# Own tiles for the retention outputs, four raw weight slots of 4 KB, and a bias table read backward in a two-layer decoder trunk

## The chip, the cores and the metric

The kernel runs on one core of a Trainium2 chip. The metric is the device time of one launch in microseconds (us), from runs on the chip. Besides those runs one execution was recorded by the hardware profiler; the times of single instructions below come from that one. The engines have short names there: PE does matmuls (PEld loads their stationary operand), DVE is the vector engine, ACT the scalar engine, POOL the general one, and SP here only issues DMAs.

## The reference

Two layers; each mixes 512 tokens of width 1024 by three causal branches (differential attention with a relative-position bias, chunked retention, a gated short convolution), gates and sums them, projects and adds; then a gated feed-forward part with a causal convolution. Cut to what the change touches:

```python
def layer(l, x):                                    # x: (512, 1024) float32
    h = rmsnorm(x, norm_mix_g[l])
    q, k, v, rq, rk, rv, rg, sb, sc, sx, gates = split(h @ w_in[l])
    # differential attention: 4 heads, 2 maps of 64 columns each, values of 128 columns
    s = q @ k.T + bias_dist[max(i - j, 0)]          # per head and map; masked where j > i
    a = softmax(s[map 0]) - lam * softmax(s[map 1])
    o_da = rmsnorm(a @ v, da_subln_g[l]) * (1 - lam_init)
    # retention: 4 heads in chunks of 128 tokens, decay per head
    o_ret = rmsnorm(retention(rotary(rq), rotary(rk), rv), ret_norm_g[l]) * silu(rg)
    o_sc = sb * causal_conv(sc * sx)
    y = sum(sigmoid(gates[b] + b_gate[b]) * (o_b @ w_branch_b) for b, o_b in enumerate((o_da, o_ret, o_sc)))
    x = x + y @ w_out[l]
    g, u = split(rmsnorm(x, norm_ffn_g[l]) @ w_ffn_in[l])
    return x + (silu(causal_conv(g)) * u) @ w_ffn_out[l]
```

`bias_dist` has one value for each distance and head; it comes from a table of 32 buckets that both layers share.

## The kernel before

**Numbers.** Every matrix product is computed from float32 operands split into a rounded part `hi` and a remainder `lo` (type float32r). One product is three matmuls: hi by hi, hi by lo, lo by hi (`mm3`, L157 to L161). A weight tile is loaded by SP into a slot of the tag "raw" (`load_w`), copied by ACT to `hi` (L150) and subtracted by DVE to `lo` (L151) (`split_w`); the slot is free again when DVE has read it. Two raw slots of 8 KB per partition exist, whatever the size of the load.

**Slots.** Tiles with one tag share a fixed number of slots in SBUF; a new tile takes the slot that comes free and its first writer waits for the last reader of the tile before. The tag "N" has nine slots (`NN`) of 4 KB and holds, over the mixing part of a layer, most of what lives long: the natural-order queries and keys of a head (`nat`), its values split in two (`v`), its transposed queries (`q`) and keys (`k`), the outputs of the heads (`om`), of retention (`omr`) and of the short convolution (`oms`), and retention's own operands (`rv`, `rT`, `knh`, `knl`). PSUM has eight banks, four under the tag "main" (projections and branch products) and four under "aux" (transposes, scores, values).

**The work of a layer.** `mix` first computes two projections of 1024 columns in natural order (`pnrqk`, `pnrvg`), then runs two things woven into each other. One is a filler of plain matmuls (`filler`): for each head h its projection into the four main banks (`pnh0` to `pnh3`, `head_chunk`), with short-convolution and gate products between them (`ptsc`, `ptg`), and the branch products `pb`. `evacuate` empties the four banks of a head: ACT copies queries and keys to `nat` (L432), squares them in place (L433) and writes the high part of the values `v` (L169), and DVE writes their low part (L170) and a row sum (L435, `msqk`). The other is attention and retention, step by step: for a block i of 128 queries the scores `pS0hi` and `pS1hi` (map 0 and 1 of head h; L487, L488), on DVE the addition of the bias with the minimum over the row (L492), on ACT the exponential (L493), on DVE the difference of the two maps, on PE the transposition `pThi` (L511), its split into `aT` by ACT (L166) and DVE (L167), and on PE the products with the values, into `po0h` for blocks 0 and 1 and `po2h` for blocks 2 and 3 (L523, L524). When the four blocks of head h are done, their normed sum `o` is transposed (`ptoh`) and stored as `om[h]`. For retention `por` stands for the products with the values and `PT` for its transposed scores.

The names in the profile carry no buffer numbers, and the names in the order rows below do (`pnh3L_2044`); in `po02` the first digit is the block and the second the head, in `pS123` the digits are map, head and block, in `pT20` head and block, and L ends the name of the tile of a layer.

**The order of instructions** on each engine is set by the framework's scheduler when the kernel is built: it takes the instructions in an order of priorities and of its own estimate of when operands and slots come free. `high_priority` puts weight loads and splits early. So a change of slots changes the order in which the engines do their work, though the source is the same. SP, POOL and each other engine then work strictly in that order: an instruction that waits holds all that is behind it on its engine.

**The bias table.** `biases` (once) builds on PE one line of 640 values per head by a product of the 32 buckets with a one-hot matrix, stores it in DRAM (`line`) and then writes it 128 times into a DRAM table `skew`, by a DMA that POOL issues (L224). `tables` (each layer) loads from `skew`, with a row pitch one shorter, the tile `bias_t`: for each query row of a block and each head 512 biases, descending in distance from left to right. The scores of block i add its last (i+1)·128 columns.

**The feed-forward part** has 22 tiles of 128 columns, in groups of 5, 9 and 8. The first group (`plain`) loads 1 MB per tile and uses it in two halves, every second block of 512 columns for g, the others for u. The other two groups (`seven`) use seven products of quarter size, for which DVE builds sums of the weight quarters (`s31`, `s24`).

Of the kernel before, what the change touches and what calls it, by code (L numbers as in the profile page):

```python
# [11 lines left out]
F32 = mybir.dt.float32  # L12
F32R = mybir.dt.float32r
I32 = mybir.dt.int32
AF = mybir.ActivationFunctionType
ALU = mybir.AluOpType
# [10 lines left out]
H = 4  # L27
# [26 lines left out]
def trunk(ctx, tc, xT, wr, wh, wt, wda, wret, wsc, wo, wf, w2, par, lamp, relb, onehot, mask, rope, gtab, out):  # L54
# [76 lines left out]
        return i  # L131

    def load_w(src, name):
        n = src.shape[1]
        with tc.high_priority():
            raw = wp.tile([P, n], F32, tag="raw", bufs=2, name="raw_" + name, padded_shape=[P, 2 * D])
            ordered(nc.sync.dma_start(raw, src))
        return raw

    def split_w(raw, name):  # L140
# [64 lines left out]
        nc.sync.dma_start(gtab_t, gtab)  # L205
        nc.sync.dma_start(mask_t, mask)

    skew = dr.tile([H, P * 640], F32, name="skew")

    def biases():  # L210

        rb = cp.tile([BUCKETS + 1, 16], F32, name="rb")[:, :H]
        V.memset(rb[BUCKETS : BUCKETS + 1], -BIG)
        G.dma_start(rb[:BUCKETS], relb)
        line = dr.tile([H, 640], F32, name="line")
        for a, b in ((0, 512), (512, 640)):
            oh = temp(f"oh{a}", b - a)[: BUCKETS + 1]
            G.dma_start(oh, onehot[:, a:b])
            ps = aux(f"psb{a}")
            T.matmul(ps[:H, : b - a], rb, oh, start=True, stop=True)  # L220
            row = temp(f"line{a}", b - a)[:H]
            V.tensor_copy(row, ps[:H, : b - a])
            G.dma_start(line[:, a:b], row)
        G.dma_start(skew.rearrange("h (p n) -> h p n", n=640), line.unsqueeze(1).broadcast_to([H, P, 640]))  # L224


    pads = [cp.tile([P, S + 2], F32, name=f"pad{i}") for i in range(2)]
# [71 lines left out]
    def mix(l, mp):  # L299
# [11 lines left out]
        for t in qz:  # L311
            G.memset(t.bitcast(F32), 0.0)

        def tables():

            src = skew[:, 127 : 127 + 639 * P].rearrange("h (p n) -> p h n", n=639)
            G.dma_start(bias_t, src[:, :, :S])

        lam_init = 0.8 - 0.6 * math.exp(-0.3 * l)

# [130 lines left out]
        def attention(h):  # L451
# [27 lines left out]
            def scores(i):  # L479
                W = (i + 1) * P  # L480
                nm = f"{h}{i}{L}"
                qs = slice(i * P, (i + 1) * P)
                z = small(2, f"z{nm}")
                e = []
                pS2 = [aux(f"pS{m}{nm}") for m in range(2)]
                for m in range(2):
                    T.matmul(pS2[m][:, :W], qs2[:, m, qs], kh2[:, m, :W], start=True, stop=False)  # L487
                    T.matmul(pS2[m][:, :W], qs2[:, m, qs], klz[:, m, :W], start=False, stop=True)  # L488
                for m, pS in enumerate(pS2):
                    s_ = temp(f"s{m}{nm}", W)  # L490
                    mn = small(1, f"mn{m}{nm}")
                    V.tensor_tensor_reduce(s_, pS[:, :W], bias_t[:, h, S - W : S], 1.0, 3.0e38, ALU.add, ALU.min, mn)  # L492
                    A.activation(s_, s_, AF.Exp, bias=mn, scale=-1.0, accum_out=z[:, m : m + 1])  # L493
                    e.append(s_)
                st_[i].update(z=z, e=e)
# [63 lines left out]
        def retention(p):  # L559
# [83 lines left out]
            yield  # L643
            yield
            ps = transposes(lambda st: o[:, st * P : (st + 1) * P], f"ptor{p}{L}")
            om[4 + p] = split2(ps, pairN(f"omr{p}{L}"), pt[:, G_RET : G_RET + 1])
            yield


# [91 lines left out]
    def ffn(l, fp):  # L741
# [28 lines left out]
            split(flat(t), flat(X[k][:, 0, 3:7]), flat(X[k][:, 1, 3:7]))  # L770

        def plain(f):
            raw = load_w(wf[l, f], f"f{L}{f}").rearrange("p (b n) -> p b n", n=S)
            ps = main(f"pg{f}{L}")
            project(xg, ps, split_w(raw[:, 1::2], f"fg{L}{f}"))
            if not norm:
                norm.append(norm_x(f"f{L}")[1])
            padt = pads[f % 2]
            V.tensor_tensor(padt[:, 2 : S + 2], ps, norm[0], ALU.mult)
            c = temp(f"c{f}{L}")  # L780
            wc = FF_W + 3 * f
            conv(c, padt, lambda t: pt[:, wc + t : wc + t + 1], pt[:, FF_B + f : FF_B + f + 1])
            A.activation(c, c, AF.Silu)
            ps = main(f"pu{f}{L}")
            project(xg, ps, split_w(raw[:, 0::2], f"fu{L}{f}"))
            u = temp(f"u{f}{L}")
            V.tensor_tensor(u, ps, norm[0], ALU.mult)
            V.tensor_tensor(u, u, c, ALU.mult)
            return split2(u, pairN(f"act{f}{L}"))

        def seven(f):
            raw = load_w(wf[l, f], f"f{L}{f}")
            r4 = raw.rearrange("p (b n) -> p b n", n=S)
            a11, a12 = r4[:, 1], r4[:, 3]
            with tc.high_priority():
                w11 = split_w(raw[:, S : 2 * S], f"fa{L}{f}")
                s31 = fp.tile([P, 2, S], F32, tag="sum", name=f"s31{f}{L}", bufs=2)
                V.tensor_tensor(s31, r4[:, 0:1].broadcast_to([P, 2, S]), r4[:, 1:3], ALU.add)
                h31, l31 = slotX(f"h31{f}{L}"), slotX(f"l31{f}{L}")
                split(s31, h31, l31)  # L800
                s24 = fp.tile([P, 2, S], F32, tag="sum", name=f"s24{f}{L}", bufs=2)
                V.tensor_tensor(s24[:, 0], s31[:, 1], a11, ALU.add)
                V.tensor_tensor(s24[:, 1], s24[:, 0], a12, ALU.add)
                h24, l24 = slotX(f"h24{f}{L}"), slotX(f"l24{f}{L}")
                split(s24, h24, l24)
                w2212 = split_w(raw[:, 2 * S : 4 * S], f"fb{L}{f}")
            w22, w12 = [tuple(t[:, b * S : (b + 1) * S] for t in w2212) for b in range(2)]

            def product(o, w, b, start, stop):
                for k in range(KT // 2):  # L810
                    sl = slice(k * P, (k + 1) * P)
                    mm3(o, (w[0][:, sl], w[1][:, sl]), (X[k][:, 0, b], X[k][:, 1, b]), start and k == 0, stop and k == KT // 2 - 1, True)

            a = main(f"pa{f}{L}")[:, :HALF]
            b = main(f"pb{f}{L}")
            padt = pads[f % 2]
            u = temp(f"u{f}{L}")
            product(a, w11, 0, True, True)
            A.copy(padt[:, 2 : HALF + 2], a)
            product(b[:, HALF:], (h31[:, 1], l31[:, 1]), 3, True, True)  # L820
            A.copy(u[:, HALF:], b[:, HALF:])
            product(a, (h24[:, 0], l24[:, 0]), 4, False, True)
            A.copy(padt[:, HALF + 2 : S + 2], a)
            product(b[:, HALF:], (h24[:, 1], l24[:, 1]), 2, False, True)
            product(a, (h31[:, 0], l31[:, 0]), 5, False, True)
            V.tensor_tensor(u[:, HALF:], u[:, HALF:], a, ALU.add)
            product(b[:, :HALF], w12, 1, False, True)
            V.tensor_tensor(padt[:, 2 : S + 2], padt[:, 2 : S + 2], b, ALU.add)
            product(a, w22, 6, False, True)
            A.copy(u[:, :HALF], a)  # L830
            c = temp(f"c{f}{L}")
            wc = FF_W + 3 * f
            conv(c, padt, lambda t: pt[:, wc + t : wc + t + 1], pt[:, FF_B + f : FF_B + f + 1])
            A.activation(c, c, AF.Silu)
            V.tensor_tensor(u, u, c, ALU.mult)
            return split2(u, pairN(f"act{f}{L}"))
# [34 lines left out]
def _consts():  # L871

    f = np.float32
    onehot = np.zeros((BUCKETS + 1, 640), f)
    half = BUCKETS // 2
    for n in range(640):
        dist = 511 - n
        if dist < 0:
            onehot[BUCKETS, n] = -1.0
            continue  # L880
        b = dist
        if dist >= half:
            b = half + int(math.log(dist / half) / math.log(MAX_DIST / half) * (BUCKETS - half))
            b = min(b, BUCKETS - 1)
        onehot[b, n] = -1.0
    inv = (f(10000.0) ** (-np.arange(32, dtype=f) / f(32))).astype(f)
    ang = (np.arange(S, dtype=f)[:, None] * inv[None, :]).astype(f).astype(np.float64)
    cs, sn = np.cos(ang), np.sin(ang)
    table = np.stack([np.concatenate([cs, cs], 1), np.concatenate([-sn, sn], 1)], 0).astype(f)
    rope = np.ascontiguousarray(table.reshape(2, ST, P, 64).transpose(2, 0, 1, 3))  # L890

    mask = (np.arange(P)[None, :] >= np.arange(P)[:, None]).astype(f)
    pos = np.arange(S, dtype=np.float64)
    gtab = np.zeros((P, ST, 4, 2), f)
    for c in range(4):
        for b in range(2):
            g = np.float64(np.log1p(-(2.0 ** (-5.0 - (2 * (c % 2) + b)))))
            col = np.exp(g * pos) if c < 2 else np.exp(-g * pos) / 8.0
            gtab[:, :, c, b] = col.reshape(ST, P).T
    return onehot, mask, rope, gtab.reshape(P, ST, 8)  # L900
# [74 lines left out]
```

## Time and profile before

| what | value |
|---|---|
| median of 3 runs | 1548.77 us (1547.65 to 1552.67) |
| the profiled execution | 1550.88 us |
| its span, first to last instruction | 1549.1 us |
| mean granted TensorE clock | 0.993 of full speed |
| DVE busy in the span | 1101.2 us (71%), 2040 instructions |
| ACT busy in the span | 731.9 us (47%), 1304 instructions |
| POOL busy in the span | 14.1 us (1%), 27 instructions |
| DMA traffic | 148.54 MB, mean 96 GB/s |

The span is 1.8 us shorter than the profiled execution's own time, since that has a start and an end outside the first and the last instruction. Rows of the trace that follow have a start and a duration in us, the engine, the line, the operation, output and inputs and shapes; a bracket at the end of a row tells how long the engine was idle before it and which instruction ended that. The ends of matmuls in the trace are modelled: two that follow each other overlap, so the pace of PE is read from the starts.

### The profile page before, as it was taken

Reading aid. Unit: us, or ns where it says so; the run is one execution under the profiler, and the core shown is the slowest. Engines: PE = TensorE matmul, PEld = TensorE weight load, DVE = VectorE, ACT = ScalarE, POOL = GpSimd, SP = SyncE. Lnnn points to the kernel's source line nnn. Section 1 sums busy time; section 2 is a strip of 40 time slices with the busy share of each in tenths; the row PEclk is TensorE's granted clock in tenths of the full one; section 3 lists DMA queues with packets and bytes.
Section 4 is the critical chain, followed back from the end, with each engine's and each line's share of the span. In section 5 each row is a group of like instructions: output and inputs, shape, how many; then the busy total and the mean of one; then the engine's idle time right before and its main releaser. Section 6 shows DMA issues by size and latency. Waiting matters only on the chain.

```text
span 1549.1 us, 21866 instructions
## 1 busy us (share of the span) xinstructions
PE 1526.5 (99%) x8510; PEld 1345.9 (87%) x8510; DVE 1101.2 (71%) x2040; ACT 731.9 (47%) x1304; POOL 14.1 (1%) x27
## 2 busy tenths in 40 slices
PE   9999989999999999999999999899999999999998
PEld 7899878888887999899789999688888879988997
DVE  7588776655569996597666887665546789957963
ACT  4456555433344564365425565453334446634641
POOL 1000000000000000000100000000000000000000
PEclk9999999999999999999999999899999999999999
DMA  5322222232221332331322222222323132224213
GB/s 188 116 103 63 88 74 84 85 98 96 98 88 55 142 110 69 136 137 55 129 82 92 72 89 72 68 81 90 102 76 123 68 110 110 92 84 165 96 45 106
DMA packets 43287, 148.54 MB, mean 96 GB/s; under 512 B 5703, under 2 KB 6102, under 8 KB 37552
## 3 DMA queue, kind: packets, MB, share of 16 engines
q1 hardware_dynamic: 41328, 143.37, 27.7%
q0 software_dynamic: 1856, 3.77, 0.7%
q8 instruction: 67, 1.10, 0.3%
q14 instruction: 36, 0.29, 0.1%
HBM read 145.01 MB, written 3.42 MB: 96 GB/s over the span
## 4 chain that ended last, share of the span: by engine, by line
PE 92%; DVE 3%; DMA 2%; ACT 2%; issue 1%; SPq 0%; ACTq 0%; DVEq 0%
PE pnrvgL L161 1%; PE pnrvgL L159 1%; PE pnrvgL L160 1%; PE pnrqkL L160 1%; PE pnrqkL L161 1%; PE pnrqkL L159 1%; PE pnh2L L161 1%; PE pnh2L L160 1%; PE pnh2L L159 1%; PE pnh1L L161 1%; PE pnh1L L160 1%; PE pnh1L L159 1%; PE pnh0L L160 1%; PE pnh0L L159 1%; PE pnh0L L161 1%
## 5 line engine op out<-in xcount | busy, mean ns | idle before, releaser
L150 ACT CAST hi_tL<-raw_tL 128x1024 fp32r<-128x1024 f32 x60 | 62.9, 1049 | 135.0 <-DMA raw_tL<-in_wt 18.3
L150 ACT CAST hi_w2L<-raw_w2L 128x640 fp32r<-128x640 f32 (+2 forms) x64 | 49.4, 781 | 97.8 <-DMA raw_w2L<-in_w 49.8
L151 DVE TENSOR_TENSOR lo_tL<-raw_tL,hi_tL 128x1024 fp32r<-128x1024 f32 x60 | 73.4, 1224 | 19.0 <-ACT hi_tL L150 18.8
L151 DVE TENSOR_TENSOR lo_w2L<-raw_w2L,hi_w2L 128x640 fp32r<-128x640 f32 (+2 forms) x64 | 56.2, 889 | 37.8 <-ACT hi_w2L L150 35.7
L150 ACT CAST hi_fbL<-raw_fL 128x1024 fp32r<-128x1024 f32 x34 | 35.7, 1051 | 26.2 <-PE p216L L160 11.7
L150 ACT CAST hi_oL<-raw_oL 128x1024 fp32r<-128x1024 f32 x16 | 16.9, 1054 | 58.1 <-issue 19.5
L151 DVE TENSOR_TENSOR lo_fbL<-raw_fL,hi_fbL 128x1024 fp32r<-128x1024 f32 x34 | 41.6, 1222 | 1.7 <-ACT hi_fbL L150 1.6
L150 ACT CAST hi_faL<-raw_fL 128x512 fp32r<-128x512 f32 x34 | 21.1, 622 | 30.9 <-DMA raw_fL<-in_wf 26.8
L151 DVE TENSOR_TENSOR lo_fuL<-raw_fL,hi_fuL 128x1024 fp32r<-128x1024 f32 x10 | 12.2, 1224 | 19.6 <-ACT hi_fuL L150 19.6
L150 ACT CAST hi_fuL<-raw_fL 128x1024 fp32r<-128x1024 f32 x10 | 10.5, 1051 | 31.2 <-PE pg0L L160 11.0
L151 DVE TENSOR_TENSOR lo_faL<-raw_fL,hi_faL 128x512 fp32r<-128x512 f32 x34 | 23.4, 689 | 0.3
L150 ACT CAST hi_nrvgL<-raw_nrvgL 128x1024 fp32r<-128x1024 f32 x8 | 8.4, 1051 | 31.5 <-PE pnrvgL L161 13.5
L150 ACT CAST hi_fgL<-raw_fL 128x1024 fp32r<-128x1024 f32 x10 | 10.5, 1054 | 24.1 <-issue 9.5
L151 DVE TENSOR_TENSOR lo_oL<-raw_oL,hi_oL 128x1024 fp32r<-128x1024 f32 x16 | 19.6, 1224 | 2.8 <-ACT hi_oL L150 2.8
L151 DVE TENSOR_TENSOR lo_nrvgL<-raw_nrvgL,hi_nrvgL 128x1024 fp32r<-128x1024 f32 x8 | 9.8, 1224 | 12.6 <-ACT hi_nrvgL L150 12.6
L151 DVE TENSOR_TENSOR lo_nh0L<-raw_nh0L,hi_nh0L 128x768 fp32r<-128x768 f32 x8 | 7.7, 958 | 13.4 <-ACT hi_nh0L L150 13.4
L150 ACT CAST hi_nrqkL<-raw_nrqkL 128x1024 fp32r<-128x1024 f32 (+1 forms) x9 | 8.6, 953 | 16.1 <-issue 11.1
L150 ACT CAST hi_bdL<-raw_bdL 128x512 fp32r<-128x512 f32 x16 | 9.9, 618 | 10.7 <-PE pb50L L160 2.2
L151 DVE TENSOR_TENSOR lo_nrqkL<-raw_nrqkL,hi_nrqkL 128x1024 fp32r<-128x1024 f32 (+1 forms) x9 | 9.9, 1105 | 7.0 <-ACT hi_nrqkL L150 7.0
L150 ACT CAST hi_nh0L<-raw_nh0L 128x768 fp32r<-128x768 f32 x8 | 6.7, 838 | 15.4 <-PE pnh0L L161 7.8
L151 DVE TENSOR_TENSOR lo_fgL<-raw_fL,hi_fgL 128x1024 fp32r<-128x1024 f32 x10 | 12.2, 1222 | 2.1 <-ACT hi_fgL L150 2.1
L150 ACT CAST hi_nh3L<-raw_nh3L 128x768 fp32r<-128x768 f32 x8 | 6.7, 835 | 14.0 <-PE ptg17L L160 7.3
(8455 smaller groups left out, 5985.4 us busy)
## 6 DMA issues: line engine op xcount, KB each, us to landing
raw_fL<-in_wf SPq DMA_DIRECT2D x44, 1024.0 KB, 4.8
raw_tL<-in_wt SPq DMA_DIRECT2D x60, 512.0 KB, 3.3
raw_w2L<-in_w SPq DMA_DIRECT2D x32, 320.0 KB, 2.9
raw_oL<-in_wo SPq DMA_DIRECT2D x16, 512.0 KB, 3.3
raw_w2L<-in_w SPq DMA_DIRECT2D x16, 512.0 KB, 3.5
raw_nrvgL<-in_wr SPq DMA_DIRECT2D x8, 512.0 KB, 3.2
raw_bdL<-in_wda SPq DMA_DIRECT2D x16, 256.0 KB, 2.6
raw_w2L<-in_w SPq DMA_DIRECT2D x16, 256.0 KB, 2.6
```

What stands on the lines that cost most here:

```text
L150: A.copy(h, raw)
L151: V.tensor_tensor(w, raw, h.bitcast(F32), ALU.subtract)
L159: T.matmul(o, a[0], b[0], start=start, stop=False, skip_group_check=more)
L160: T.matmul(o, a[0], b[1], start=False, stop=False, skip_group_check=more)
L161: T.matmul(o, a[1], b[0], start=False, stop=stop, skip_group_check=more)
```

## The change

It has four parts.

1. `load_w` has four raw slots of 4 KB instead of two of 8 KB. The loads of 1 MB become two of 512 KB each: `plain` loads its two halves apart, `seven` an upper and a lower half. Since the lower and the upper half are two tiles now, the sum `s31` is two additions of 512 columns instead of one of 1024, 34 more DVE instructions in all. SP has 44 more DMAs.
2. The outputs of retention (`omr`, two per layer) have tiles of their own in the pool of the mixing part, and no longer take slots of the tag "N".
3. `skew` is gone, with its DMA. `line` is stored ascending in distance, and `bias_t` is loaded straight from it: row p of head h is the 512 values from place p on. The scores read it backward, with a step of −1 in the last dimension.
4. The one-hot matrix is numbered to match.

```diff
     def load_w(src, name):
-        n = src.shape[1]
+        n = int(np.prod(src.shape[1:]))
         with tc.high_priority():
-            raw = wp.tile([P, n], F32, tag="raw", bufs=2, name="raw_" + name, padded_shape=[P, 2 * D])
-            ordered(nc.sync.dma_start(raw, src))
+            raw = wp.tile([P, n], F32, tag="raw", bufs=4, name="raw_" + name, padded_shape=[P, D])
+            ordered(nc.sync.dma_start(raw if len(src.shape) == 2 else raw.rearrange("p (b n) -> p b n", b=src.shape[1]), src))
...
-    skew = dr.tile([H, P * 640], F32, name="skew")
+    line = dr.tile([H, 640], F32, name="line")
...
-        G.dma_start(skew.rearrange("h (p n) -> h p n", n=640), line.unsqueeze(1).broadcast_to([H, P, 640]))
...
+        def back(h, n):
+
+            at = bias_t[:, h, n - 1 : n]
+            return bass.AP(at.tensor, at.offset, [at.ap[0], (-1, n)])
...
-            src = skew[:, 127 : 127 + 639 * P].rearrange("h (p n) -> p h n", n=639)
-            G.dma_start(bias_t, src[:, :, :S])
+            at = line[:, 0:1]
+            G.dma_start(bias_t, bass.AP(at.tensor, at.offset, [[1, P], [640, H], [1, S]]))
...
-                    V.tensor_tensor_reduce(s_, pS[:, :W], bias_t[:, h, S - W : S], 1.0, 3.0e38, ALU.add, ALU.min, mn)
+                    V.tensor_tensor_reduce(s_, pS[:, :W], back(h, W), 1.0, 3.0e38, ALU.add, ALU.min, mn)
...
-            om[4 + p] = split2(ps, pairN(f"omr{p}{L}"), pt[:, G_RET : G_RET + 1])
+            om[4 + p] = split2(ps, mp.tile([P, 2, S], F32R, name=f"omr{p}{L}"), pt[:, G_RET : G_RET + 1])
...
-            raw = load_w(wf[l, f], f"f{L}{f}").rearrange("p (b n) -> p b n", n=S)
+            both = wf[l, f].rearrange("p (b n) -> p b n", n=S)
             ps = main(f"pg{f}{L}")
-            project(xg, ps, split_w(raw[:, 1::2], f"fg{L}{f}"))
+            project(xg, ps, split_w(load_w(both[:, 1::2], f"fg{L}{f}"), f"fg{L}{f}"))
...
-            project(xg, ps, split_w(raw[:, 0::2], f"fu{L}{f}"))
+            project(xg, ps, split_w(load_w(both[:, 0::2], f"fu{L}{f}"), f"fu{L}{f}"))
...
-            raw = load_w(wf[l, f], f"f{L}{f}")
-            r4 = raw.rearrange("p (b n) -> p b n", n=S)
-            a11, a12 = r4[:, 1], r4[:, 3]
+            upper, lower = [load_w(wf[l, f, :, b * D : (b + 1) * D], f"f{b}{L}{f}") for b in range(2)]
+            a21, a11, a22, a12 = upper[:, :S], upper[:, S:], lower[:, :S], lower[:, S:]
...
-                V.tensor_tensor(s31, r4[:, 0:1].broadcast_to([P, 2, S]), r4[:, 1:3], ALU.add)
+                V.tensor_tensor(s31[:, 0], a21, a11, ALU.add)
+                V.tensor_tensor(s31[:, 1], a21, a22, ALU.add)
...
-        dist = 511 - n
+        dist = n - 127
```

The slots decide the order. Before, the values of head 3 (`v3`) take the slot of the keys of head 2 (`k2`) in the tag "N", and head 1's output takes that of head 2's queries; now `v3` takes the slot of `nat2`. The two places in the program below are in layer 0, and layer 1 has the same order at both.

On PE before, this is where the last scores of head 2 are made and the first filler matmul (`pb22`, a branch product that needs a main bank) follows:

```order
L487 MATMUL pS023L_2355<-k2L_1934,q2L_1933 128x512
L488 MATMUL pS023L_2355<-klzL_122,q2L_1933 128x512
L523 MATMUL po02L_2192<-v2L_1562,aT21L_2274 128x256
L524 MATMUL po02L_2192<-v2L_1562,aT21L_2274 128x128
L523 MATMUL po02L_2192<-v2L_1562,aT21L_2274 128x256
L524 MATMUL po02L_2192<-v2L_1562,aT21L_2274 128x128
L487 MATMUL pS123L_2356<-k2L_1934,q2L_1933 128x512
L488 MATMUL pS123L_2356<-klzL_122,q2L_1933 128x512
L511 MATMUL pT22L_2369<-ident,s022L_2263 128x128 x3
L159 MATMUL pb22L_2300<-oms0L_1034,hi_b2L_2296 128x512
```

Ahead of these rows stand, in this order, the last matmul of head 3's projection, `pT20`, the first pair of `po02`, four transposes `pto1`, four matmuls for the scores of block 2 and two transposes `pT21`. On PE of the change, the end of head 3's projection (`pnh3`) is:

```order
L159 MATMUL pnh3L_2040<-hi_nh3L_2198,xs7mL_233 128x384
L160 MATMUL pnh3L_2040<-lo_nh3L_2199,xs7mL_233 128x384
L514 MATMUL pT20L_2150<-ident,s020L_2028 128x128
L161 MATMUL pnh3L_2040<-hi_nh3L_2198,xs7mL_233 128x384
L159 MATMUL pnh3L_2041<-hi_nh3L_2198,xs6mL_230 128x384
```

and, after 8 more matmuls of `pnh3`,

```order
L159 MATMUL pnh3L_2042<-hi_nh3L_2198,xs7mL_233 128x384
L160 MATMUL pnh3L_2042<-lo_nh3L_2199,xs7mL_233 128x384
L161 MATMUL pnh3L_2042<-hi_nh3L_2198,xs7mL_233 128x384
L526 MATMUL po02L_2190<-v2L_1560,aT20L_2152 128x256
L527 MATMUL po02L_2190<-v2L_1560,aT20L_2152 128x128
L159 MATMUL pb22L_2298<-oms0L_1032,hi_b2L_2294 128x512
L160 MATMUL pb22L_2298<-oms0L_1032,hi_b2L_2294 128x512
L161 MATMUL pb22L_2298<-oms0L_1032,lo_b2L_2295 128x512
```

`pT20` has moved ahead by 13 matmuls of 384 columns: it stood directly ahead of `po02`. `pb22` has moved from behind the last scores of head 2 to directly behind `po02`; `pto1` and the scores of blocks 2 and 3 of head 2 now stand inside a gate product that comes later (`ptg20`).

On ACT, in the same stretch, the rows before end with the values of head 3 behind the work for head 2's blocks 1 and 3:

```order
L493 ACTIVATE s122L_2267,z22L_2256<-s122L_2267,mn122L_2268 128x384
L166 CAST aT21L_2274<-pT21L_2271 128x256
L493 ACTIVATE s023L_2361,z23L_2354<-s023L_2361,mn023L_2362 128x512
L525 COPY o2L_2020<-po02L_2192 128x128
L169 ACTIVATE v3L_2039<-pnh3L_2041,rmL_298 128x128
```

and of the change:

```order
L435 COPY nat3L_2036<-pnh3L_2039 128x256
L436 ACTIVATE pnh3L_2039<-pnh3L_2039 128x256
L166 CAST aT20L_2152<-pT20L_2150 128x128
L169 ACTIVATE v3L_2037<-pnh3L_2039,rmL_298 128x128
L435 COPY nat3L_2036<-pnh3L_2040 128x256
L436 ACTIVATE pnh3L_2040<-pnh3L_2040 128x256
L169 ACTIVATE v3L_2037<-pnh3L_2040,rmL_298 128x128
```

The values of each bank of head 3 are written right behind the copy and the square of that bank.

On SP, at the start of the program, before:

```order
L198 DMA x_85<-in_xT 128x512
L204 DMA par_111<-in_par 128x140
L205 DMA gtab_t<-in_gtab 128x32
L206 DMA mask_t<-in_mask 128x128
L380 DMA ropeL_126<-in_rope 128x512
L137 DMA raw_nrqkL_182<-in_wr 128x1024
L198 DMA x_86<-in_xT 128x512
```

and of the change:

```order
L198 DMA x_85<-in_xT 128x512
L137 DMA raw_nrqkL_182<-in_wr 128x1024
L198 DMA x_86<-in_xT 128x512
L198 DMA x_87<-in_xT 128x512
L198 DMA x_88<-in_xT 128x512
L198 DMA x_89<-in_xT 128x512
L137 DMA raw_nrqkL_222<-in_wr 128x1024
L137 DMA raw_nrqkL_328<-in_wr 128x1024
```

The third weight load has moved ahead of the four constants, which now follow among the next loads.

More of the change, by code (lines that the diff above doesn't have):

```diff
@@ L214, in biases @@
         G.dma_start(rb[:BUCKETS], relb)
-        line = dr.tile([H, 640], F32, name="line")
         for a, b in ((0, 512), (512, 640)):
@@ L791, in seven @@
         def seven(f):
-            raw = load_w(wf[l, f], f"f{L}{f}")
-            r4 = raw.rearrange("p (b n) -> p b n", n=S)
-            a11, a12 = r4[:, 1], r4[:, 3]
+            upper, lower = [load_w(wf[l, f, :, b * D : (b + 1) * D], f"f{b}{L}{f}") for b in range(2)]
+            a21, a11, a22, a12 = upper[:, :S], upper[:, S:], lower[:, :S], lower[:, S:]
             with tc.high_priority():
-                w11 = split_w(raw[:, S : 2 * S], f"fa{L}{f}")
+                w11 = split_w(a11, f"fa{L}{f}")
                 s31 = fp.tile([P, 2, S], F32, tag="sum", name=f"s31{f}{L}", bufs=2)
-                V.tensor_tensor(s31, r4[:, 0:1].broadcast_to([P, 2, S]), r4[:, 1:3], ALU.add)
+                V.tensor_tensor(s31[:, 0], a21, a11, ALU.add)
+                V.tensor_tensor(s31[:, 1], a21, a22, ALU.add)
                 h31, l31 = slotX(f"h31{f}{L}"), slotX(f"l31{f}{L}")
@@ L805, in seven @@
                 split(s24, h24, l24)
-                w2212 = split_w(raw[:, 2 * S : 4 * S], f"fb{L}{f}")
+                w2212 = split_w(lower, f"fb{L}{f}")
             w22, w12 = [tuple(t[:, b * S : (b + 1) * S] for t in w2212) for b in range(2)]
```

## The prediction

> **What bounds the kernel now.** I read the page first: busy time by engine, and the shares of the chain of work that ended last.
>
> ```profile
> span 1549.1 us, 21866 instructions
> PE 1526.5 (99%) x8510; PEld 1345.9 (87%) x8510; DVE 1101.2 (71%) x2040; ACT 731.9 (47%) x1304; POOL 14.1 (1%) x27
> PE 92%; DVE 3%; DMA 2%; ACT 2%; issue 1%; SPq 0%; ACTq 0%; DVEq 0%
> ```
>
> PE is the bound, and the change takes no matmul away. So it can only win what PE loses: idle time, and time at a lower clock. The view of PE's waits lists the first kind (engine, line, what it waited for, us in total, times, longest):
>
> ```profile
> PE po02L L523 <- ACT aT20L L166: 3.9, 2, 2.0
> PE pto1L L284 <- DVE o1L L544: 2.7, 2, 1.4
> PE pb22L L159 <- DVE msqk3L L435: 2.2, 2, 1.4
> PE por00L L617 <- ACT PT00L L166: 1.8, 1, 1.8
> ```
>
> The three rows besides `por00` come twice, once in each layer, all at the end of head 3's projection. The view by windows shows these places (window, its length, busy time of PE, PEld, DVE, ACT and POOL, then granted clock, DMA share, GB/s):
>
> ```profile
> 206.20:219.00 12.80, 6.73 (x26) 3.99 (x24) 8.95 (x35) 7.39 (x25) 0.00 (x0) 0.87 0.19 56
> 971.10:984.00 12.90, 8.13 (x26) 5.16 (x24) 9.00 (x35) 7.49 (x25) 0.00 (x0) 0.67 0.15 56
> 984.00:989.20 5.20, 5.17 (x12) 4.11 (x13) 5.10 (x18) 1.44 (x5) 0.00 (x0) 0.51 0.00 0
> 975.50:989.10 13.60, 12.16 (x33) 8.78 (x34) 10.20 (x35) 6.12 (x20) 0.00 (x0) 0.50 0.05 19
> 77.80:81.20 3.40, 3.40 (x15) 3.01 (x13) 3.34 (x9) 3.35 (x10) 0.00 (x0) 0.50 0.83 320
> ```
>
> The first two are layers 0 and 1: 26 matmuls in nearly 13 us. In layer 1 the clock stays at half for 13.6 us; the last window is the half clock behind the wait of `por00`. What stands in the first one, from PE's timeline and one row of ACT's:
>
> ```profile
> 206.19 0.27 PE L511 MATMUL pT20L<-ident,s020L 128*128 128x128 f32 x1
> 208.45 0.39 PE L523 MATMUL po02L<-v2L,aT20L 128*128 128x256 f32 x1 [1.99 <-ACT aT20L L166]
> 209.55 0.33 PE L524 MATMUL po02L<-v2L,aT20L 128*128 128x128 f32 x1 [0.71 <-DVE aT20L L167]
> 211.25 1.09 PE L284 MATMUL pto1L<-ident,o1L 128*128 128x128 f32 x4 [1.37 <-DVE o1L L544]
> 216.55 0.40 PE L488 MATMUL pS123L<-klzL,q2L 128*128 128x512 f32 x1
> 219.00 0.50 PE L159 MATMUL pb22L<-oms0L,hi_b2L 128*128 128x512 f32 x1 [1.44 <-DVE msqk3L L435]
> 217.32 1.14 ACT L169 ACTIVATE v3L<-pnh3L,rmL 128x128 fp32r<-128x128 f32 x4
> ```
>
> `pb22` is the first matmul that is not attention's. It needs a main bank; the banks hold head 3's projection until ACT writes `v3` at 217.32, and `v3` sits in the slot of `k2`, last read by the scores `pS123`, which run until 216.9. So PE must walk through head 2's chain of small dependent steps first, bare, with nothing to put between them.
>
> **The stall at head 3 (own tiles for `omr`).** The order rows show `v3` out of `k2`'s slot and `pb22` straight behind `po02`. The work in the stretch is not saved, only its gaps. Its pace, from two rows of the chain (start, duration, four instructions each):
>
> ```profile
> 19.61 0.91 PE pnrqkL L159 x4
> 55.40 0.44 PE ptr0L L284 x4
> ```
>
> A matmul of 512 columns takes 0.91/4 = 0.228 us, a transpose 0.11. The stretch holds 10 transposes (1.1 us), four scores of 384 and four of 512 columns and three pairs of `po02` of 384 (4736 columns, 4736/512 × 0.228 = 2.1): 3.2 us in all. Layer 0 loses 12.8 − 3.2 = **9.6**. Layer 1 loses 12.9 − 3.2 = 9.7, and as the clock stays at half to 989.2 another 5.2 × 0.49 = 2.5: **12.2**. What is late next? `po02` stays behind `pT20`, now with 13 matmuls of 384 columns between, 13 × 0.17 = 2.2 us. Before, the way through both halves of the split took from 206.19 to the end of this row:
>
> ```profile
> 209.21 0.28 DVE L167 TENSOR_TENSOR aT20L<-pT20L,aT20L 128x128 fp32r<-128x128 f32 x1
> ```
>
> that is 3.3 us. Uncovered: at most 1.1 per layer, at least 0 (ACT and DVE may be less crowded). I take 0.5, **+1.0** for two layers. `pto1` and head 2's later scores stand inside a gate product, whose matmuls cover them.
>
> **The wait of `por00` (four slots, no `skew`).** Rows of POOL, the chain, ACT and PE:
>
> ```profile
> 55.31 1.15 POOL L224 DMA_DIRECT2D skew<-line  x1 [2.20 <-DMA line<-line]
> 65.79 7.35 DMA raw_tL<-in_wt
> 73.24 1.05 ACT L150 CAST hi_tL<-raw_tL 128x1024 fp32r<-128x1024 f32 x1 [5.92 <-DMA raw_tL<-in_wt]
> 76.85 0.33 PE L617 MATMUL por00L<-rv0L,PT00L 128*128 128x128 f32 x1 [1.82 <-ACT PT00L L166]
> raw_tL<-in_wt SPq DMA_DIRECT2D x60, 512.0 KB, 3.3
> skew<-line POOLq DMA_DIRECT2D x1, 1280.0 KB, 19.5
> ```
>
> A weight load that starts when its slot comes free, while `skew` is written, needs 7.35 us where such loads take 3.3 (the last two rows: KB and median us to landing); ACT waits 5.92 for it, and PT00 behind it in ACT's order comes late. Two more slots let the load start earlier, and `skew` is gone. PE gets back 1.8 of wait, and half of the 3.4 us at clock 0.50: **3.5**. Next in line is ACT's own work, which the bound below takes in.
>
> On the clock, the Trainium skill's page "TensorE: Matmul & The Clock Gate", section "HAM oscillation — how this bites in real kernels", asks for "no PE-idle gaps >~3.4µs". The trace differs: half clock followed single waits of 1.8 and 2.0 us. By that rule this term would be 1.8 alone, and the sum 1.7 less.
>
> **The start.** The third weight load waits for one of two slots:
>
> ```profile
> 7.06 0.33 SPq L137 DMA_DIRECT2D raw_nrqkL<-in_wr  x1
> 12.39 1.04 ACT L150 CAST hi_nrqkL<-raw_nrqkL 128x1024 fp32r<-128x1024 f32 x1 [0.70 <-DMA raw_nrqkL<-in_wr]
> 13.48 1.19 PE L159 MATMUL pnrqkL<-hi_nrqkL,xs2mL 128*128 128x512 f32 x4 [1.13 <-ACT hi_nrqkL L150]
> ```
>
> With a third slot it is issued ahead of the constants. ACT idles 0.70 for it and is busy ahead of that: **0.7**, between 0 and PE's 1.13.
>
> **Costed at nothing.** Rows of DVE by source, of windows, of POOL and of DMAs:
>
> ```profile
> L492 DVE CUSTOM_DVE_ANT_0 s000L<-pS000L,biasL x2: 291/292/292, 115.4 to 880.4; 128x128 f32<-128x128 f32 x2
> L492 DVE CUSTOM_DVE_ANT_0 s003L<-pS003L,biasL x2: 680/681/682, 143.6 to 908.6; 128x512 f32<-128x512 f32 x2
> L798 DVE TENSOR_TENSOR s316L<-raw_fL x2: 1221/1222/1224, 517.8 to 1283.8; 128x1024 f32<-128x1024 f32 x2
> L802 DVE TENSOR_TENSOR s246L<-s316L,raw_fL x2: 684/684/685, 520.9 to 1287.3; 128x512 f32<-128x512 f32 x2
> 115.00:300.00 185.00, 178.93 (x931) 156.01 (x931) 138.13 (x393) 100.79 (x238) 0.00 (x0) 0.99 0.24 78
> 880.00:1060.00 180.00, 175.20 (x898) 152.78 (x898) 132.09 (x374) 99.08 (x236) 0.00 (x0) 0.96 0.23 74
> 650.00:700.00 50.00, 50.00 (x407) 49.49 (x406) 48.95 (x63) 31.53 (x52) 0.00 (x0) 1.00 0.36 127
> 742.89 0.76 POOL L317 DMA_DIRECT2D biasL<-skew  x1
> biasL<-skew POOLq DMA_DIRECT2D x2, 1024.0 KB, 7.3
> ```
>
> *The sum `s31`.* Two additions of 512 for one of 1024: 2 × 0.684 − 1.222 = 0.15 us on DVE, 34 times, 5 us if all of it came out, which is this edit's upper bound. Even where DVE is fullest (650 to 700) it has 1.05 us idle in 50, some 0.2 per tile of about 10 us, and PE is at 50.00: hidden, barely.
>
> *Smaller, more numerous loads.* 44 more issues on SP, which waits on slots more than it works (0.33 us each); each load of 512 KB lands in 3.3 us (the row of `raw_t` above), and four can be under way where a tile of the feed-forward part takes some 10 us and needs two. No cost; lost cover would show as PE waits on the split weights, 3.3 at most where a group of tiles begins.
>
> *The direct bias load.* Between the 7.3 us of today's load and the 19.5 of `skew`; `line` has landed at 55.31, the first use is at 115.4, so 60 us cover either. In layer 1 it is issued at 742.89 and used at 880.4. There a memset ahead of it on POOL gets a wait for PE and DVE, with this load and the one of lambda queued behind it; 137 us cover that.
>
> *The backward read.* No row has a negative step. Lower end: nothing. Upper end: as if twice the columns went through, 1.222 − 0.684 = 0.54 us per 512 columns. A layer reads 4 heads × 2 maps × 1280 = 10,240 columns, so up to 20 × 0.54 = 10.8 us more DVE time. From 115 to 300 DVE idles 185.0 − 138.1 = 46.9, in layer 1 47.9. I take nothing, nearest to the forward row of the same instruction, and keep 10.8 as the far end.
>
> Against this part speaks the Trainium skill's "Vector Engine (DVE) Microarchitecture Reference", section "5.2 Measured stream behaviour on trn2 (trn3 not measured)": a port has its full rate only on runs of at least two adjacent 4-byte words that start on an 8-byte boundary, and its worst single steps cost 2.50 ns per column against 1.05. Negative steps the page leaves unmeasured. By its worst step the estimate is 10,240 × 1.45 ns = 14.8 us of DVE per layer; no run here shows it yet.
>
> **The sum.** −9.6 − 12.2 + 1.0 − 3.5 − 0.7 = −25.0. It stands against the profiled execution, 1550.88 (1.8 us of it outside the span): 1525.9. That execution lay 2.1 above the median 1548.77 of the runs shown, so **1523.8**, given as 1524.
>
> **Rivals.**
>
> *B, a shorter bare wait stays.* `po02`, or `pb22` behind a bank not yet emptied, still waits 1 to 2 us, and half clock follows, as it did behind `por00`'s 1.8. For it: the 2.2 us of cover against 3.3. Against: `pb22` needs only the first of four banks. Price: in layer 0 1.0 of wait and 1.7 of clock, in layer 1 1.0 and half of 13.6, 10.5 in all where I have 1.0: 1533.5. The skill's clock rule would leave only the waits, 1525.
>
> *C, the backward read is slow and half exposed.* Of 10.8 per layer half comes out, since the additions stand between scores and exponentials: 1524 + 10.8 = 1535. Against: the idle time above, and filler matmuls.
>
> *C', the other side.* The same instruction, but so slow that DVE becomes the bound of attention. Forward it costs 10,240 × 0.681/512 = 13.6 us a layer. It passes DVE's idle time at 47/13.6 = 3.5 times more, and eats the gain of 25, 12.5 a layer, at (47 + 12.5)/13.6 = 4.4 times more, so at 5.4 times its duration. At 6 times: 2 × (68 − 47) = 42 more, 1566. Against: no row of DVE comes near such a ratio.
>
> *D, the stall stays.* `v3` still waits, now for the last reader of `nat2`, or scores and banks tie up another way, and only `por00` and the start are won: 1548.8 − 4.2 = 1544.6. Against: the order rows put `v3` between the copies of head 3's banks on ACT.
>
> **Chances.** Forecast 0.66 (1520 to 1528: the `po02` wait 0 to 2.1, the start 0 to 1.1, scatter of the runs), B 0.15, C 0.10, D 0.06, C' 0.03. Faster by over 0.3% (under 1544.1; about what a measurement of this kernel can tell from no change) are the forecast, B and C: 0.91. D is the same, 0.06; C' slower, 0.03. The range 1520 to 1537 takes in the forecast, B, C and the bound of `s31`; what lies outside is D, C' and some 0.05 of unforeseen new waits.
>
> **What would show it.** Right: the profile after has no PE wait of over 1 us on `po02`, `pto1` and `pb22`, no clock under 0.9 in either stretch, `v3` on ACT between head 3's copies, no wait on PT00, and L492 near 0.68 at 512 columns. B shows as a wait there with half clock behind it; C as L492 nearer 1.2 and PE waits on scores; `s31` as PE waits on `l31` or `h24` in the feed-forward part. Wrong would be: new waits elsewhere that the new order of the whole program makes, which no row of before can show.

## The result, and the profile after

The changed kernel takes 1524.58 us (median of 4 runs, 1523.98 to 1525.18), the kernel before 1550.24 (4 runs, 1547.65 to 1552.67): a ratio of 0.9835, 95% interval 0.9816 to 0.9854. The forecast was 1524 in a range of 1520 to 1537. The profiled execution took 1523.98 us, 26.9 less than the one before.

From the page of the changed kernel, the rows that answer to those of before:

```profile
span 1522.2 us, 22065 instructions
...
PE 1513.5 (99%) x8510; PEld 1339.4 (88%) x8510; DVE 1103.4 (72%) x2074; ACT 733.5 (48%) x1304; POOL 13.0 (1%) x26
...
PE 96%; DVE 2%; DMA 1%; issue 0%; ACT 0%; SPq 0%; ACTq 0%; DVEq 0%
```

PE has the same 8510 matmuls and is busy 13 us less. Most of that is half clock: the kernel before had 20.5 us of it ahead of its last matmul, with PE busy for 18.6 of them, and half of that, some 9 us, is the estimate of what full clock saves; the rest was not followed up. PE's share of the chain rose from 92% to 96%. PE's waits of over 0.3 us, the whole list of the changed kernel:

```profile
PE p204L L159 <- ACT hi_w2L L150: 1.6, 2, 0.8
PE ps_warm L190 <- POOL ones L184: 1.1, 1, 1.1
PE pa5L L159 <- ACT pad L822: 0.6, 1, 0.6
PE p224L L159 <- ACT hi_w2L L150: 0.4, 2, 0.2
PE p225L L159 <- ACT hi_w2L L150: 0.4, 2, 0.2
```

`po02`, `pto1`, `pb22` and `por00` are gone from it. Windows as long as the two stalls and the half clock behind `por00` were, laid on the same places of the changed kernel:

```profile
199.00:211.80 12.80, 12.80 (x65) 11.13 (x64) 11.64 (x37) 7.52 (x21) 0.00 (x0) 1.00 0.25 85
952.90:965.80 12.90, 12.90 (x66) 11.20 (x65) 11.49 (x37) 7.30 (x20) 0.00 (x0) 1.00 0.24 82
73.00:76.40 3.40, 3.40 (x29) 3.23 (x27) 3.17 (x8) 3.35 (x9) 0.00 (x0) 1.00 0.00 0
```

65 and 66 matmuls stand where 26 did, at full clock. Where the time came from is read by following the same matmul through both traces: its start in each, the lead of the changed kernel there, and what was won since the row above.

| matmul (start in the trace) | before | after | lead | won here |
|---|---|---|---|---|
| last of `pnrvg`, layer 0 | 55.01 | 53.87 | 1.1 | 1.1, the start |
| first of `por01`, layer 0 | 86.10 | 81.35 | 4.8 | 3.6, `por00` |
| first of `pb00`, layer 0 | 324.42 | 309.99 | 14.4 | 9.7, head 3 |
| last of `p227`, layer 0 | 778.52 | 762.91 | 15.6 | 1.2, the feed-forward part |
| first of `pb00`, layer 1 | 1091.80 | 1064.10 | 27.7 | 12.1, head 3 |
| last of `p227`, layer 1 | 1545.01 | 1517.85 | 27.2 | −0.5, the feed-forward part |

The rows at the two places, of the changed kernel's timeline, first PE, then ACT and DVE:

```profile
199.00 0.27 PE L514 MATMUL pT20L<-ident,s020L 128*128 128x128 f32 x1
...
201.36 0.28 PE L526 MATMUL po02L<-v2L,aT20L 128*128 128x256 f32 x1
...
201.54 0.45 PE L159 MATMUL pb22L<-oms0L,hi_b2L 128*128 128x512 f32 x1
...
199.31 0.27 ACT L166 CAST aT20L<-pT20L 128x128 fp32r<-128x128 f32 x1
199.47 0.38 ACT L169 ACTIVATE v3L<-pnh3L,rmL 128x128 fp32r<-128x128 f32 x1
...
200.05 0.28 DVE L167 TENSOR_TENSOR aT20L<-pT20L,aT20L 128x128 fp32r<-128x128 f32 x1
...
67.68 1.05 ACT L150 CAST hi_tL<-raw_tL 128x1024 fp32r<-128x1024 f32 x1 [2.76 <-PE pnh0L L161]
...
73.76 0.23 PE L620 MATMUL por00L<-rv0L,PT00L 128*128 128x128 f32 x1
```

`v3` is written at 199.47, while head 3's projection still runs, and `pb22` follows `po02` without a gap. In the last two rows ACT waits for a slot of split weights and no longer for a load, and `por00` has no bracket.

### The profile page after: what moved, and what is told of

Its sections match the earlier page's. It is cut to its first block, busy times and chain, and to the rows that moved or that the text cites. A ratio compares the mean times of both kernels' runs of the same rounds, so it can differ in the third digit from the quotient of the medians.

```text
span 1522.2 us, 22065 instructions
## 1 busy us (share of the span) xinstructions
PE 1513.5 (99%) x8510; PEld 1339.4 (88%) x8510; DVE 1103.4 (72%) x2074; ACT 733.5 (48%) x1304; POOL 13.0 (1%) x26
## 4 chain that ended last, share of the span: by engine, by line
PE 96%; DVE 2%; DMA 1%; issue 0%; ACT 0%; SPq 0%; ACTq 0%; DVEq 0%
PE pnrvgL L161 1%; PE pnrvgL L159 1%; PE pnrvgL L160 1%; PE pnrqkL L160 1%; PE pnrqkL L161 1%; PE pnrqkL L159 1%; PE pnh2L L161 1%; PE pnh2L L159 1%; PE pnh3L L160 1%; PE pnh3L L161 1%; PE pnh1L L161 1%; PE pnh2L L160 1%; PE pnh3L L159 1%; PE pnh1L L160 1%; PE pnh0L L159 1%; PE pnh1L L159 1%
## 5 line engine op out<-in xcount | busy, mean ns | idle before, releaser
L151 DVE TENSOR_TENSOR lo_tL<-raw_tL,hi_tL 128x1024 fp32r<-128x1024 f32 x60 | 73.4, 1223 | 15.9 <-ACT hi_tL L150 15.6
L150 ACT CAST hi_fbL<-raw_f1L 128x1024 fp32r<-128x1024 f32 x34 | 35.7, 1050 | 38.8 <-PE pa8L L160 6.8
L151 DVE TENSOR_TENSOR lo_fbL<-raw_f1L,hi_fbL 128x1024 fp32r<-128x1024 f32 x34 | 41.4, 1219 | 5.1 <-ACT hi_fbL L150 5.0
L150 ACT CAST hi_faL<-raw_f0L 128x512 fp32r<-128x512 f32 x34 | 21.1, 622 | 28.1 <-DMA raw_f0L<-in_wf 10.0
L151 DVE TENSOR_TENSOR lo_fuL<-raw_fuL,hi_fuL 128x1024 fp32r<-128x1024 f32 x10 | 12.2, 1223 | 19.6 <-ACT hi_fuL L150 19.6
L151 DVE TENSOR_TENSOR lo_faL<-raw_f0L,hi_faL 128x512 fp32r<-128x512 f32 x34 | 23.3, 684 | 3.7 <-ACT hi_faL L150 3.7
L150 ACT CAST hi_fuL<-raw_fuL 128x1024 fp32r<-128x1024 f32 x10 | 10.5, 1051 | 31.1 <-issue 17.5
L150 ACT CAST hi_fgL<-raw_fgL 128x1024 fp32r<-128x1024 f32 x10 | 10.5, 1054 | 24.1 <-issue 16.0
L151 DVE TENSOR_TENSOR lo_fgL<-raw_fgL,hi_fgL 128x1024 fp32r<-128x1024 f32 x10 | 12.2, 1221 | 2.2 <-ACT hi_fgL L150 2.2
```

The source lines that it names most:

```text
L150: A.copy(h, raw)
L151: V.tensor_tensor(w, raw, h.bitcast(F32), ALU.subtract)
```

## The experiments

Eight kernels were run, each with three rounds against the kernel before.

### Only the own tiles

```diff
-            om[4 + p] = split2(ps, pairN(f"omr{p}{L}"), pt[:, G_RET : G_RET + 1])
+            om[4 + p] = split2(ps, mp.tile([P, 2, S], F32R, name=f"omr{p}{L}"), pt[:, G_RET : G_RET + 1])
```

> Only the own tiles for omr; raw slots, skew and the forward bias stay as before. Theory (v3 sat in the slot of k2, and that alone made both stalls at head 3): both stalls go, 9.7 + 12.1 = 21.8 us less than before; the wait of por00 (1.8 us) and the half clock behind it stay. Rival (the four raw slots carry part of it, since the weights of pb22 and ptg19 come earlier): half of that or less, with PE waiting on hi_t or hi_b2 at 200 to 220 us.

Measured: 1527.99 us against 1549.99, ratio 0.9856 (0.9841 to 0.9871), 22.0 us less. The first row of this kernel's PE waits:

```profile
PE por00L L617 <- ACT PT00L L166: 1.9, 1, 1.9
```

Both stalls are gone (9.6 and 12.0 us by the starts of `pb00`), with nothing of the weights in the way; the wait of `por00` stays. The theory's number held. That `v3` alone made the stalls this run can't show, since two tiles less in the tag "N" move other slots as well. One more thing differed: no half clock followed the wait this time, of which more below.

### Only the four raw slots, and only the bias part

The first of these is the kernel before with the change's `load_w`, `plain` and `seven`, the second the kernel before with its `line`, `tables`, `back` and the one-hot matrix.

> Only the four raw slots of 4 KB and the split loads. Theory: start 1.1 us earlier, por00's wait gone (its load starts some 10 us earlier, so that it lands in time even beside the skew DMA): 4.7 us less than before; both stalls at head 3 stay. Rival (it was the skew DMA that delayed the load, and four loads beside it share the same rate): only 1.1 us less, the wait of 1.8 us on PT00 stays.

> Only the bias part: no skew DMA, line ascending, direct load, backward read. Theory: without skew the load ahead of PT00 takes 3.3 instead of 7.35 us, 4 us earlier, more than the wait of 1.8: por00's wait and its half clock go, 3.5 us less than before; the backward read costs nothing. Rival 1 (slots cause it, not the DMA): 0. Rival 2 (backward read costs): some us more on DVE, row of 512 columns over 0.69 us.

Measured: slots 1543.6 us, ratio 0.9955 (0.9940 to 0.9969); bias part 1548.58, ratio 0.9985 (0.9974 to 0.9996). The largest PE waits of the first, then of the second kernel:

```profile
PE po02L L523 <- ACT aT20L L166: 2.9, 2, 1.5
PE pto1L L284 <- DVE o1L L544: 1.7, 2, 0.9
```

```profile
PE po02L L526 <- ACT aT20L L166: 4.2, 2, 2.1
PE pto1L L282 <- DVE o1L L547: 2.7, 2, 1.4
```

`por00` is in neither list. By the start of `por01` both won 3.6 us there, so either edit alone is enough, and the change pays for it twice. The slots won more than the 4.7 expected, since the stalls at head 3 shrank as well, by 1.6 and 1.1 us by the starts of `pb00` (2.9 us against 3.9 on `aT20`). The bias part won less than the 3.5: in its trace the lead of 4.1 at `por01` is down to 2.3 behind the stall of layer 0, which has more half clock than before (6.8 and 3.4 us where the window of before, 0.87 over 12.8 us, makes 3.3):

```profile
205.06:211.89 6.83, 4.97 (x14) 3.26 (x14) 3.72 (x18) 2.37 (x8) 0.00 (x0) 0.50 0.14 38
215.30:218.71 3.41, 3.41 (x9) 2.64 (x10) 3.41 (x13) 1.32 (x5) 0.00 (x0) 0.50 0.00 0
```

### One wait put back: v3 behind k2

The changed kernel, with one slot for the keys of head 2 and the values of head 3.

```diff
+            v = mp.tile([P, 2, S], F32R, tag="hold", name=f"v{h}{L}", bufs=1) if h == 3 else pairN(f"v{h}{L}")
...
+            qs2, kh2 = pairN(f"q{h}{L}"), mp.tile([P, 2, S], F32R, tag="hold", name=f"k{h}{L}", bufs=1) if h == 2 else pairN(f"k{h}{L}")
...
+            om[4 + p] = split2(ps, pairN(f"omr{p}{L}") if p else mp.tile([P, 2, S], F32R, name=f"omr{p}{L}"), pt[:, G_RET : G_RET + 1])
```

> The changed kernel, but the values of head 3 share one slot with the keys of head 2 again (a tag of its own with one slot; omr1 goes back to the tag N for the space). Theory: both stalls at head 3 come back and nothing else, 9.7 + 12.1 = 21.8 us slower than the changed kernel, so 3 to 5 us under before, with half clock in layer 1. Rival (the stall came from the other slots or the crowded order, not from this one wait): within 5 us of the changed kernel.

Measured: 1533.26 us, ratio 0.9893 (0.9878 to 0.9908): only 8.7 us above the changed kernel, not 21.8. The wait is there: ACT writes all four parts of `v3` right behind the scores `pS123`. A row of ACT's timeline, a window around it, and PE's three largest waits in total:

```profile
206.22 1.14 ACT L169 ACTIVATE v3L<-pnh3L,rmL 128x128 fp32r<-128x128 f32 x4 [0.19 <-PE pS123L L490]
```

```profile
201.00:213.00 12.00, 9.31 (x46) 7.22 (x45) 11.29 (x40) 7.68 (x24) 0.00 (x0) 1.00 0.27 88
```

```profile
PE pT21L L514 <- DVE mn022L L495: 2.5, 2, 1.4
PE pb22L L159 <- DVE msqk3L L438: 2.2, 2, 1.1
PE pa5L L159 <- ACT pad L822: 2.2, 2, 1.6
```

At head 3 it costs 3.6 us in layer 0 and 3.7 in layer 1 (by the starts of `pb00`), without half clock in this trace, where the old stalls cost 9.7 and 12.1. The rest of the 8.7 lies in the feed-forward part, where `pa5` waits 2.2 us against 0.6 in the changed kernel. That `omr1` went back to the tag "N" costs nothing by itself, as the last run below shows. In this kernel `pT20` still stands 13 matmuls ahead of `po02`, so the waits on `aT20` are missing. The theory of one wait fell: something else had put head 2's chain late.

### The second wait: om0 behind k1

The traces name a candidate. Before, head 1's keys `k1` and head 0's output `om0` shared a slot; their rows, and the beginnings of head 3's projection and of head 2's transposes:

```profile
184.37 0.33 PE L159 MATMUL pnh3L<-hi_nh3L,xs0mL 128*128 128x384 f32 x1
...
187.75 0.45 PE L487 MATMUL pS113L<-k1L,q1L 128*128 128x512 f32 x1
...
188.24 0.69 ACT L169 ACTIVATE om0L<-pto0L,par 128x512 fp32r<-128x512 f32 x1
...
192.42 0.27 PE L284 MATMUL pt02L<-ident,nat2L 128*128 128x128 f32 x1
```

and in the changed kernel:

```profile
172.59 0.69 ACT L169 ACTIVATE om0L<-pto0L,par 128x512 fp32r<-128x512 f32 x1
...
178.81 0.40 PE L490 MATMUL pS113L<-k1L,q1L 128*128 128x512 f32 x1
...
179.97 0.34 PE L159 MATMUL pnh3L<-hi_nh3L,xs0mL 128*128 128x384 f32 x1
...
183.33 0.38 PE L282 MATMUL pt02L<-ident,nat2L 128*128 128x128 f32 x2
```

Before, `om0` is written only behind the last scores of head 1, and head 2 begins 8.1 us after head 3's projection does; now `om0` is written 6 us ahead of those scores, and head 2 begins after 3.4 us. Two kernels put this wait back, alone and together with that of `v3`.

```diff
+            qs2, kh2 = pairN(f"q{h}{L}"), mp.tile([P, 2, S], F32R, tag="holdk", name=f"k{h}{L}", bufs=1) if h == 1 else pairN(f"k{h}{L}")
...
+            om[h] = split2(ps, pairN(f"om{h}{L}") if h else mp.tile([P, 2, S], F32R, tag="holdk", name=f"om{h}{L}", bufs=1), pt[:, G_SUB : G_SUB + 1])
```

> The changed kernel, but the output of head 0 (om0) shares one slot with the keys of head 1 (k1), as before the change; omr1 goes back to the tag N for the space. om0 then waits for the last scores of head 1, with its transposes pto0 in a bank of PSUM, and head 2 begins some 4.7 us later against head 3's projection. Theory (two slot waits make the stall, and this one only puts head 2 late, while filler matmuls stay free to run): within 2 us of the changed kernel, no PE wait over 1 us at head 3. Rival (head 2's late begin is the larger part of the stall by itself): 10 to 14 us slower than the changed kernel, with waits on aT20 and o1.

> The changed kernel with both slot waits back: om0 in the slot of k1, and v3 in the slot of k2; omr0 and omr1 in the tag N. Theory (the two together are the old stall): waits of PE on aT20, o1 and msqk3 as in the run with the four raw slots alone, half clock behind them in layer 1, and 19 us slower than the changed kernel (9.6 - 1.5 in layer 0 and 12.1 - 1.0 in layer 1, by that run), so about 1543 to 1544. Rival (the two waits only add up): the 8.7 us of v3's wait alone plus what om0's alone gives, 9 to 11 us, 1534 to 1536.

Measured: `om0` alone 1525.45 us, ratio 0.9842 (0.9828 to 0.9857), within 1 us of the changed kernel; both together 1539.71, ratio 0.9936 (0.9921 to 0.9951), 15.1 above it.

With `om0` alone the wait is there: `om0` is written at 183.48, behind the start of `pS113` at 182.99, and head 2 begins 7.0 us after head 3's projection. But `pb22` now runs ahead of `po02`, and its six matmuls cover the split of `pT20`:

```profile
202.76 0.47 PE L159 MATMUL pb22L<-oms0L,hi_b2L 128*128 128x512 f32 x1
...
204.23 0.28 PE L526 MATMUL po02L<-v2L,aT20L 128*128 128x256 f32 x1
```

PE's largest waits at head 3 with both, then ACT's row of `v3` and the half clock of layer 1:

```profile
PE po02L L526 <- ACT aT20L L166: 2.9, 2, 1.5
...
PE po02L L527 <- DVE aT20L L167: 1.4, 2, 0.7
PE pb22L L159 <- DVE msqk3L L438: 1.2, 1, 1.2
...
PE pto1L L282 <- DVE o1L L547: 0.9, 2, 0.5
```

```profile
209.50 1.14 ACT L169 ACTIVATE v3L<-pnh3L,rmL 128x128 fp32r<-128x128 f32 x4 [0.67 <-PE pS123L L490]
```

```profile
966.93:970.35 3.42, 3.33 (x12) 2.36 (x11) 2.08 (x6) 2.58 (x7) 0.00 (x0) 0.50 0.34 129
```

With both, the waits on `aT20` of the run with the four slots alone are back to the digit; those on `o1` are 0.9 against 1.7. So the two waits don't add up (0.9 and 8.7 against 15.1): a late head 2 costs next to nothing while filler matmuls may run, and a `v3` that blocks the banks costs little while head 2 is early; together they leave PE alone with head 2's chain. The sum fell 4 us short of the 19 expected. In layer 0 the stall is 6.7 us against some 8 in the slots-only run, in layer 1 6.7 against 11; there the half clock lasted 3.4 us here, and 13.7 in the slots-only run and in the run that follows.

The run that follows is the fairer measure: it has all but the own tiles and takes 18.3 us more than the changed kernel, of which the two waits bring back 15.1. Two things differ in what is missing. One is the shorter half clock. The other seems to be a third slot wait, which no run put back: head 1's output `om1`, before in the slot of head 2's queries. In the run that follows, as in the kernel before, it is written behind the last scores of head 2 (`pS123` at 210.18), with both waits ahead of them (208.97). First that run's row, then that with both waits:

```profile
211.88 0.70 ACT L169 ACTIVATE om1L<-pto1L,par 128x512 fp32r<-128x512 f32 x1
```

```profile
205.83 0.69 ACT L169 ACTIVATE om1L<-pto1L,par 128x512 fp32r<-128x512 f32 x1
```

How much each of the two is worth was not measured.

### Everything but the own tiles, and one own tile for two

> The changed kernel without the own tiles of omr (slots and bias part stay). Theory: slots and bias part overlap in por00's 3.6 us, so that the bias part adds only some 0.4 us at the start to the slots' 6.4: about 1543. Rival (their gains add): 1542 or less.

> The changed kernel with one own tile instead of two (omr1 in the tag N). Theory (one slot more is enough to part both om0 from k1 and v3 from k2; the slots taken are other ones): within 2 us of the changed kernel. Rival: one stall stays, 8 us or more slower.

Measured: without own tiles 1542.87 us, ratio 0.9954 (0.9940 to 0.9969); with one own tile 1525.25, ratio 0.9840 (0.9824 to 0.9857). The first is 7.3 us under its runs of before, where slots alone were 6.4: by the medians the bias part adds 0.9, more than 0.4 and less than its own 1.4, too little to tell the two readings apart. The traces do: `por00`'s 3.6 us are won once. Half clock in layer 1 of the first kernel:

```profile
966.53:980.19 13.66, 11.91 (x32) 8.49 (x33) 10.50 (x38) 6.44 (x21) 0.00 (x0) 0.50 0.12 38
```

One own tile gives what two give. The largest waits of that kernel are at the start and in the feed-forward part:

```profile
PE pnrqkL L159 <- ACT hi_nrqkL L150: 2.3, 2, 1.3
PE p204L L159 <- ACT hi_w2L L150: 1.6, 2, 0.8
```

No kernel was clearly faster than the changed one.

## Why the prediction was right, step by step

**The stalls at head 3** were forecast at 9.6 and 12.2 us and gave 9.7 and 12.1. The size was read as the length of the stretch minus the work in it at PE's pace, and that needs no cause. The cause as given, `v3` in the slot of `k2`, was only a part of it: alone that wait costs some 3.6 us a layer at head 3. The other part was `om0` in the slot of `k1`, which put head 2 some 4.7 us later (8.1 − 3.4) against head 3's projection. The prediction saw its mark, `pT20` directly ahead of `po02`, and took it for a place in the order only. Both waits together bring back 15.1 of 18.3 us; the rest stays open between half clock and `om1`. How `om0` delays `pt02` was not shown: its transposes `pto0` hold a PSUM bank until it is written, which would do it. The traces fit that: from the start of `pS013` to that of `pS113`, which needs a bank too, it takes 4.85 us before (182.90 to 187.75) and 0.78 in the changed kernel (178.03 to 178.81).

**The new wait of `po02`**, a cost of 1.0, did not come. The term was too large: it took the 3.3 us that the split of `pT20` needed before, and that held a weight cast of ACT (1.03 us) and its subtraction on DVE (1.22 us), which have nothing to do with `pT20`. Now `aT20` is complete at 200.05 + 0.28 = 200.33, 1.3 us after `pT20` starts, and the cover is 2.36.

**`por00`** was forecast at 3.5 and gave 3.6. Either edit suffices, which the prediction left open ("two more slots", "and `skew` is gone").

**The start** was forecast at 0.7 and gave 1.1 in this profile. ACT no longer waits for the third weight load, as forecast, but no run shows that this wins time. At the last `pnrvg` the profiles of the seven kernels with four slots lead by 1.2 to 0.0 us, and the two with 0.0 (`om0` alone, and one own tile) have lost that wait too; their first weights came 0.3 and 0.5 us later. The bias part alone, with two slots, leads by 0.5.

**Costed at nothing.** Rows of DVE in the changed kernel, by source, for the backward read and for `s31`:

```profile
L495 DVE CUSTOM_DVE_ANT_0 s000L<-pS000L,biasL x2: 291/292/292, 110.7 to 864.8; 128x128 f32<-128x128 f32 x2
...
L495 DVE CUSTOM_DVE_ANT_0 s003L<-pS003L,biasL x2: 677/681/685, 139.0 to 893.1; 128x512 f32<-128x512 f32 x2
```

```profile
L801 DVE TENSOR_TENSOR s316L<-raw_f0L,raw_f1L x2: 684/684/685, 496.1 to 1250.8; 128x512 f32<-128x512 f32 x2
```

The backward read costs what the forward one did, 0.292 us for 128 columns and 0.681 for 512; C and C' fall. It is a step of −1 word on one of two operands, the other in PSUM, and the penalty for single steps that the Trainium skill gives ("Vector Engine (DVE) Microarchitecture Reference", section "5.2 Measured stream behaviour on trn2 (trn3 not measured)") did not show. `s31` is two additions of 0.684, as taken. The feed-forward part won 1.2 us in layer 0 and lost 0.5 in layer 1; it was put at nothing, and by the same two starts the seven kernels with four slots won 0.3 to 1.2 in layer 0 and lost 0.0 to 1.5 in layer 1. What moves there was not followed up.

**B and D** did not come: the changed kernel has no PE wait over 0.8 us besides the warm-up's, and no half clock until its last matmul. B also took it that half clock follows a single wait of 1 to 2 us. It need not: in the kernel with the wait of `v3` alone PE waits up to 1.4 us at head 3, and no half clock follows. And the wait of 2.0 us that was named for it did not stand alone: PE was busy for 0.71 of the 3.41 us ahead of that half clock (207.48 to 210.89).

**The time.** That 1524 came so near to 1524.58 is in part luck. Between the profiled executions the change won 26.9 us where the sum was 25.0; the 1.0 for `po02` that did not come, 0.4 more at the start and 0.7 in the feed-forward part make most of the difference. The step of 2.1 down to the median of three runs hid it: with a fourth run that median is 1550.24, only 0.6 under the profiled execution.

## What to carry to other kernels

Price a stall from the stretch: its length minus the work in it at the engine's own pace, half clock included. Before naming its cause, list who held each slot before its present owner, for every tile of the chain that waits: two waits that look like one are told apart only by putting each back by itself, and may cost little alone. Where two edits remove the same wait, count it once.

## What the runs showed of the clock

Half clock came in pieces of 3.41 us: by the granted clock in the traces it lasted 3.41, 6.83 or 13.65 us (that behind the last matmul aside), and within one execution its beginnings lay whole multiples of 3.413 us apart (77.77, 210.89 and 975.48 in the kernel before: 39 and 263 pieces from the first). What counts seems to be how busy PE was in the piece before, not the length of one wait. The piece with the wait of `por00` and the one after it, in the kernel before and in the one with only the own tiles (there the pieces counted back from the half clock that begins behind its last matmul):

```profile
74.36:77.77 3.41, 1.59 (x14) 1.38 (x13) 3.41 (x9) 2.87 (x10) 0.80 (x1) 1.00 0.34 108
77.77:81.18 3.41, 3.41 (x15) 3.02 (x13) 3.35 (x9) 3.36 (x10) 0.00 (x0) 0.50 0.83 320
```

```profile
75.08:78.49 3.41, 1.53 (x12) 1.45 (x13) 3.41 (x10) 2.87 (x10) 0.80 (x1) 1.00 0.51 161
78.49:81.90 3.41, 3.41 (x22) 2.99 (x20) 3.35 (x8) 3.36 (x9) 0.00 (x0) 1.00 0.66 262
```

Nearly the same piece, 1.59 and 1.53 us busy of 3.41, was followed by half clock in one and not in the other. In the other eight profiles, the program's start and end aside, every piece at full clock that was up to 0.44 busy had half clock behind it, and none over 0.56; between these, 0.53 and 0.556 had it, 0.54 and 0.555 had not. The Trainium skill's page "TensorE: Matmul & The Clock Gate", section "HAM oscillation — how this bites in real kernels", names a window of 3.4 us and warns of idle gaps as long; the length agrees with the 3.41 here, but a piece half idle was enough. So near one half this share does not decide; whether the pieces that count lie a little otherwise, or something else takes part, the traces do not tell. A stall's price can thus differ from run to run, which would fit the spread of the kernel before: 7.6 us in 14 runs, from 1545.85 at a mean clock of 0.998 to 1553.49 at 0.990. The changed kernel, at 1.0 in all of its 4, spread over 1.2. Why half clock holds for four pieces in layer 1 (for one in the run with both waits) and for one or two at a time in layer 0 stays open.
